# Strassen's seven products for the FFN of the main tokens, with its activations in DRAM and the output projection chunk by chunk

## The chip, the cores and the metric

The kernel runs on one core of a Trainium2 chip, one launch. The metric is device microseconds (us) of that core, the median of three executions. One execution was taken by the hardware profiler; the rows below are from it. The engines are PE (TensorE matmuls; PEld is its weight load), DVE (VectorE), ACT (ScalarE), POOL (GpSimd) and SP (SyncE, which here issues the DMAs).

## What is computed

Two layers of a hybrid block over 1024 main tokens and 256 context tokens, width 1024. Cut to what matters here (g1, sc2, sh2, g2 come from the conditioning vector; the context has its own):

```
x = x + g1 * (y @ w_out[l])                              # y: the three mixers, side by side
h = rms_norm(x, g_ffn[l]) * (1.0 + sc2) + sh2
gate, val = jnp.split(h @ w_up[l], 2, axis=-1)           # 1024 -> 2 x 2816
u = silu(depthwise_conv3(gate) + b) * val                # along the tokens
x = x + g2 * (u @ w_down[l])                             # 2816 -> 1024
# the same for the context tokens, in layer 0 only
```

Ahead of this stands, in each layer, the mixer part: a norm, the combined input projection, neighbourhood attention, differential attention and a Mamba-2 scan.

## The kernel before

Activations lie with their channels on the 128 partitions: 8 blocks of channels, and tokens in three chunks: 0 and 1 (512 main tokens each) and 2 (256 context tokens). Every large product is done at fp32 precision as three matmuls, H·H, L·H and H·L: a tile is rounded to fp32r (H, by a cast) and what is left over is L (by a subtraction). For a weight block, `load_w` does this: an SP DMA into `wr`, the cast on ACT (L240, `wH`), the subtraction on POOL (L241, `wL`).

`outproj` goes chunk by chunk. It reads the mixers' output (already split) from DRAM, does 8 blocks of w_out and adds each into the resident `xt` (DVE, L1278); `norm_sq` sums the squares, and when the chunk is through, `norm_scale` makes the reciprocal root `rs` (a matmul with ones, four ACT steps, two DVE steps) and `norm_apply` makes H and L of the normalised chunk: a multiplication by `rs` on DVE (L364), scale and shift on ACT (L93), the cast on DVE (L369), the subtraction on DVE and POOL in turn (L370).

`ffn` takes two of the 22 blocks of D_FF at a time: gate product (L390 to L392, evacuated by ACT into `fpad`), the convolution on DVE (L1194, L1197), SiLU on ACT, val product and multiplication (L1206), the split into `gh`/`gl` (L1207, L1208), and then the down product of both blocks (L1232 to L1234) for 8 output blocks and each chunk, each added into `xt` by DVE (L1237). So up and down alternate, and each down group of 6 matmuls has a PSUM bank of its own (tag `mm`, 3 banks). The order of instructions on each engine is chosen at build time by the scheduler of the language, not written by hand; each engine then runs its list in order and waits where it must.

In the last pair of layer 0 the next layer's norm follows chunk by chunk.

Of the kernel before, what the change touches and what calls it, by code (L numbers as in the profile page):

```python
# [80 lines left out]
def hybrid_kernel(ctx, tc, xin, cc, w_ada, bada, gmf, w_in, w_dt, w_out, w_up, w_dn, vec, cst, rope, nab, out):  # L81
# [30 lines left out]
    ps_p = ctx.enter_context(tc.tile_pool(name="ps", bufs=1, space=PSUM))  # L112
    mmx = [None, None]

# [6 lines left out]
    open_mm(mm=3)  # L121
# [69 lines left out]
    hp = [None, None]  # L191
    w_pre = []

    def open_h(nm):
        hp[0] = ExitStack()
        hp[1] = hp[0].enter_context(tc.tile_pool(name=nm, bufs=1, side="right", reuse_waits="tile"))

# [6 lines left out]
    hxp = [None, None]  # L204

    def open_hx(nm):
        hxp[0] = ExitStack()
        hxp[1] = hxp[0].enter_context(tc.tile_pool(name=nm, bufs=1, side="right", reuse_waits="tile"))
        new_hx()

    def new_hx():
        for k in range(HX, KT):
            hH[k][0] = hxp[1].tile([128, 512], F32R, tag=f"hxH{k}", name=f"hH{k}_0")
            hL[k][0] = hxp[1].tile([128, 512], F32R, tag=f"hxL{k}", name=f"hL{k}_0")

    def new_h(ci=None, y=False):
        h_p = hp[1]
        for i, (_, n) in enumerate(ALLC):
            if ci is None or ci == i:
                if i == 0 and hxp[1] is not None and not y:  # L220
                    new_hx()
                for k in range(KT if i or hxp[1] is None else HX):
                    hH[k][i] = h_p.tile([128, n], F32R, tag=f"hH{k}_{i}", name=f"hH{k}_{i}")
                    hL[k][i] = h_p.tile([128, n], F32R, tag=f"hL{k}_{i}", name=f"hL{k}_{i}")
# [22 lines left out]
    def pst(tag, bufs):  # L247
        return ps_p.tile([128, 512], F32, tag=tag, name=tag, bufs=bufs)
# [23 lines left out]
    def ada_finish(l, s, k0, nk, pa, pool=None):  # L272
        pm = pa[:, 256:512] if nk == 2 else pst("t", 2)
        for k in range(nk):
            if k % 2 == 0:
                row = (pool or const).tile([128, 256], F32, tag="arow", name="arow", bufs=2 if pool else 1)
# [18 lines left out]
    def ada_native(pool, todo):  # L295
# [11 lines left out]
        for i, (l, s, e) in enumerate(todo):  # L307
# [8 lines left out]
            ada_finish(l, s, 2 * e, 2, pa)  # L316
# [13 lines left out]
    def norm_temps(pool):  # L330
        tl = lambda nm, n=512: pool.tile([128, n], F32, name=nm)
        return dict(acc=[tl(f"acc{i}", n) for i, (_, n) in enumerate(ALLC)], sq=[tl("sq0"), tl("sq1")],
                    rv=tl("rv"), nt=[tl(f"nt{i}") for i in range(4)])
# [19 lines left out]
    def norm_apply(tmp, l, i, xt, ci, rs=None):  # L353
# [6 lines left out]
        for k in range(KT):  # L360
            t = tmp["nt"][k % len(tmp["nt"])][:, :n]
            xv = xt[k][:, c0:c0 + n]
            if not scaled:
                V.tensor_tensor(out=t, in0=xv, in1=rs, op=ALU.mult)  # L364
                xv = t
# [117 lines left out]
    def mixer(l):  # L483
# [66 lines left out]
        with phase(f"sw{l}") as sp:  # L550
# [58 lines left out]
          if True:  # L609
# [558 lines left out]
    def ffn(l, xt):  # L1168
        full = l == 0
        chunks = ALLC if full else MAINC  # L1170
        last = l == NL - 1
        with phase(f"ffn{l}") as p:
# [4 lines left out]
            W = 1282 if full else 1024  # L1177

            def gate_ev(f):
                pad = pads[f % 2]  # L1180

                def ev(ps, c0, n):
                    o = 1 + c0 if c0 < SEQ else 1027
                    S.copy(out=pad[:, o:o + n], in_=ps)  # L1184

                return ev

            def up(f, gate_done=False):
                pad = pads[f % 2]
                if not gate_done:  # L1190
                    proj(w_up[l, 2 * f], chunks, gate_ev(f))
                a = p.tile([128, 1282], F32, tag="fa", name="fa", bufs=1)
                fw = V_FW + 3 * f
                V.tensor_scalar(out=a[:, :W], in0=pad[:, 0:W], scalar1=vcol(l, fw), scalar2=vcol(l, V_FB + f),  # L1194
                                op0=ALU.mult, op1=ALU.add)
                for j in range(1, 3):
                    V.scalar_tensor_tensor(out=a[:, :W], in0=pad[:, j:j + W], scalar=vcol(l, fw + j), in1=a[:, :W],  # L1197
                                           op0=ALU.mult, op1=ALU.add)
                act(out=a[:, :W], in_=a[:, :W], func=ACTF.Silu)
                gh = p.tile([128, T], F32R, tag="gh", name="gh", bufs=3)  # L1200
                gl = p.tile([128, T], F32R, tag="gl", name="gl", bufs=3)

                def evv(ps, c0, n):
                    o = c0 if c0 < SEQ else 1026
                    t = a[:, o:o + n]
                    V.tensor_tensor(out=t, in0=t, in1=ps, op=ALU.mult)  # L1206
                    S.copy(out=gh[:, c0:c0 + n], in_=t)  # L1207
                    G.tensor_tensor(out=gl[:, c0:c0 + n], in0=t, in1=gh[:, c0:c0 + n].bitcast(F32),  # L1208
                                    op=ALU.subtract)

                proj(w_up[l, 2 * f + 1], chunks, evv)
                return gh, gl

            def down(f0, hid, fin):
                tmp = None
                if fin and not last:
                    e0 = p.tile([128, T], F32R, tag="gh", name="gh", bufs=3).bitcast(F32)
                    e1 = p.tile([128, T], F32R, tag="gl", name="gl", bufs=3).bitcast(F32)
                    fa = p.tile([128, 1282], F32, tag="fa", name="fa", bufs=1)
                    tmp = dict(acc=[pads[0][:, 0:512], pads[0][:, 512:1024], pads[1][:, 0:256]],  # L1220
                               sq=[pads[1][:, 256:768], pads[1][:, 768:1280]], rv=fa[:, 0:512],
                               nt=[e0[:, 0:512], e1[:, 0:512], e0[:, 512:1024], e1[:, 512:1024]])
                ws = [load_w(w_dn[l, (f0 + i) * 128:(f0 + i + 1) * 128, :]) for i in range(len(hid))]
                steps = [(o, c) for o in range(KT) for c in chunks]
                if fin:
                    steps = [(o, c) for c in chunks for o in range(KT)]
                for o, (c0, n) in steps:
                    os_ = slice(o * 128, (o + 1) * 128)
                    ps = mmt()[:, :n]
                    for i, (gh, gl) in enumerate(hid):  # L1230
                        wh, wl = ws[i]
                        PE.matmul(ps, wh[:, os_], gh[:, c0:c0 + n], start=(i == 0), stop=False)  # L1232
                        PE.matmul(ps, wh[:, os_], gl[:, c0:c0 + n], start=False, stop=False)  # L1233
                        PE.matmul(ps, wl[:, os_], gh[:, c0:c0 + n], start=False, stop=(i == len(hid) - 1))  # L1234
                    w = 1 if c0 >= SEQ else 0
                    xv = xt[o][:, c0:c0 + n]
                    V.scalar_tensor_tensor(out=xv, in0=ps, scalar=mods[l][:, 5, o, w:w + 1], in1=xv,  # L1237
                                           op0=ALU.mult, op1=ALU.add)
                    if fin and last:
                        SP.dma_start(out=out[o * 128:(o + 1) * 128, c0:c0 + n], in_=xv)  # L1240
                    elif fin:
                        ci = c0 // 512
                        if o == 0 and ci == 0:
                            exp_tables()
                        norm_sq(tmp, ci, o, xv)
                        if c0 < SEQ:
                            SP.dma_start(out=xd[o, :, c0:c0 + n], in_=xv)
                        if o == 1 and ci > 0:
                            norm_apply(tmp, l + 1, 0, xt, ci - 1)
                if fin and not last:  # L1250
                    norm_apply(tmp, l + 1, 0, xt, 2)
# [202 lines left out]
```

## Time and profile before

| what | value |
|---|---|
| device time, median of 3 (range) | 3625.64 us (3623.48 to 3633.13) |
| span of the profiled execution | 3627.4 us |
| PE busy | 3433.8 us (95%), 18762 matmuls |
| PEld busy | 2724.3 us (75%) |
| DVE busy | 1950.4 us (54%) |
| ACT busy | 1242.3 us (34%) |
| POOL busy | 1446.3 us (40%) |
| DMA | 381.03 MB, mean 105 GB/s |

The profile gives no other time of the profiled execution than its span; it is 1.8 us above the median. The FFN of layer 0 runs from about 1080 to 1960 us, that of layer 1 from about 2900 to the end. A busy share is a mean over stages: PE's 95% is 100% in the FFN and less in the mixers and at the joints between the stages.

### The profile page before, as it was taken

To read this page: it belongs to the slowest core of one execution; us is meant where nothing else is said; L and a number is where in the kernel's file an instruction comes from. 1 tells how busy PE (TensorE), PEld (TensorE's weight loads), DVE (VectorE), ACT (ScalarE), POOL (GpSimd) and SP (SyncE) were. 2 spreads that over 40 slices of the span, in tenths; PEclk is the share of its full clock that TensorE was granted. 3 is DMA by queue.
4 is the path that set the end of the run, shared out by engine and by line. 5 is a ranking of instruction groups with operands and counts; after the bars stand their busy time and mean duration, and the time that the engine had idled before them with its cause. 6 is when DMAs were issued, how large, how long until landed. Compare 5 with 4: busy or idle time off the path is not lost. (4 is left out here: it accounts for less than half of the span.)

```text
span 3627.4 us, 49090 instructions
## 1 busy us (share of the span) xinstructions
PE 3433.8 (95%) x18762; PEld 2724.3 (75%) x18762; DVE 1950.4 (54%) x3816; ACT 1242.3 (34%) x2159; POOL 1446.3 (40%) x1092
## 2 busy tenths in 40 slices
PE   7998898899899999999999898998999999999999
PEld 3876676666678888888887676776666777887887
DVE  6735875787373343333335744885784633334333
ACT  4232433777341111111113333344675421221211
POOL 2136563666362222222222326673565532322332
PEclk8999999999999999999999999998999999999999
DMA  8255444753721111111112236447656211111111
GB/s 294 98 199 164 131 126 132 191 152 105 244 83 46 35 41 35 37 39 36 35 35 82 69 114 211 128 128 192 167 156 215 77 53 41 53 47 41 53 47 70
DMA packets 260202, 381.03 MB, mean 105 GB/s; under 512 B 20736, under 2 KB 161152, under 8 KB 259712
## 3 DMA queue, kind: packets, MB, share of 16 engines
q1 hardware_dynamic: 259968, 377.90, 33.8%
q8 instruction: 148, 2.42, 0.3%
q14 instruction: 86, 0.70, 0.1%
HBM read 294.72 MB, written 83.10 MB: 104 GB/s over the span
## 5 line engine op out<-in xcount | busy, mean ns | idle before, releaser
L390 PE MATMUL mm<-hH,wH 128*128 128x512 f32 (+1 forms) x2960 | 1117.6, 379 | 34.2 <-ACT wH L240 7.6
L391 PE MATMUL mm<-hL,wH 128*128 128x512 f32 (+1 forms) x2960 | 1113.2, 376 | 9.5 <-POOL hL L370 5.3
L392 PE MATMUL mm<-hH,wL 128*128 128x512 f32 (+1 forms) x2960 | 1111.4, 376 | 6.2 <-POOL wL L241 6.2
L241 POOL TENSOR_TENSOR wL<-wr,wH 128x1024 fp32r<-128x1024 f32 x220 | 533.2, 2429 | 1218.4 <-ACT wH L240 1195.3
L390 PEld LDWEIGHTS mm<-hH,wH 128*128 128x128 f32 x2960 | 564.7, 191 | 157.6 <-issue 15.1
L391 PEld LDWEIGHTS mm<-hL,wH 128*128 128x128 f32 x2960 | 564.4, 191 | 127.4 <-POOL hL L370 7.8
L392 PEld LDWEIGHTS mm<-hH,wL 128*128 128x128 f32 x2960 | 564.4, 191 | 114.8 <-POOL wL L241 7.7
L240 ACT CAST wH<-wr 128x1024 fp32r<-128x1024 f32 x220 | 228.3, 1048 | 808.1 <-PE mm L1233 471.9
L1237 DVE SCALAR_TENSOR_TENSOR xt<-mm,mods,xt 128x512 f32<-128x512 f32 (+1 forms) x440 | 300.9, 697 | 253.6 <-PE mm L1234 253.1
L1194 DVE TENSOR_SCALAR fa<-fpad,vc 128x1282 f32<-128x1282 f32 (+1 forms) x44 | 111.1, 2526 | 558.6 <-ACT fpad L1184 550.9
L1234 PE MATMUL mm<-gh,wL 128*128 128x512 f32 (+1 forms) x880 | 328.9, 374 | 0.0
L1232 PE MATMUL mm<-gh,wH 128*128 128x512 f32 (+1 forms) x880 | 325.0, 375 | 3.7 <-DVE xt L1237 3.6
L1233 PE MATMUL mm<-gl,wH 128*128 128x512 f32 (+1 forms) x880 | 326.9, 372 | 0.0
L720 DVE TENSOR_SCALAR_CACHE_REDUCE e<-s 128x512 f32<-128x512 f32 (+1 forms) x400 | 228.4, 588 | 88.2 <-PE s L719 85.6
L1208 POOL TENSOR_TENSOR gl<-fa,gh 128x512 fp32r<-128x512 f32 (+1 forms) x110 | 127.6, 1160 | 300.7 <-ACT gh L1207 300.7
L93 ACT ACTIVATE e<-e,nm 128x1280 f32<-128x1280 f32 (+1 forms) x144 | 182.9, 1271 | 53.6 <-DVE nm L723 48.5
L719 PE MATMUL s<-ks,qst 128*128 128x512 f32 (+1 forms) x400 | 161.5, 441 | 39.0 <-DVE e L720 23.4
L1232 PEld LDWEIGHTS mm<-gh,wH 128*128 128x128 f32 x880 | 164.5, 188 | 41.1 <-DVE xt L1237 8.7
L738 POOL TENSOR_TENSOR e<-e 128x1280 f32<-128x1280 f32 (+1 forms) x72 | 193.1, 2684 | 3.4
L1233 PEld LDWEIGHTS mm<-gl,wH 128*128 128x128 f32 x880 | 165.3, 188 | 32.7 <-issue 0.2
L1234 PEld LDWEIGHTS mm<-gh,wL 128*128 128x128 f32 x880 | 165.5, 188 | 32.1
L1206 DVE TENSOR_TENSOR fa<-fa,mm 128x512 f32<-128x512 f32 (+1 forms) x110 | 69.8, 635 | 209.3 <-PE mm L392 151.7
(269 smaller groups left out, 4930.1 us busy)
## 6 DMA issues: line engine op xcount, KB each, us to landing
wr<-in_w_up_dram SPq DMA_DIRECT2D x88, 512.0 KB
wa<-in_w_ada_dram SPq DMA_DIRECT2D x56, 512.0 KB
wr<-in_w_in_dram SPq DMA_DIRECT2D x48, 512.0 KB
wr<-in_w_dn_dram SPq DMA_DIRECT2D x44, 512.0 KB
wr<-in_w_ada_dram SPq DMA_DIRECT2D x40, 512.0 KB
wr<-in_w_out_dram SPq DMA_DIRECT2D x40, 512.0 KB
nbt<-in_nab_dram SPq DMA_DIRECT2D x64, 192.0 KB
ks<-qkd SPq DMA_DIRECT2D x16, 640.0 KB
```

The costliest lines, as they stand in the source:

```text
L93: ins = S.activation(**kw)
L240: S.copy(out=wh, in_=wr)
L241: (eng or G).tensor_tensor(out=wl, in0=wr, in1=wh.bitcast(F32), op=ALU.subtract)
L390: PE.matmul(ps[:, :n], wh[:, ks], r, start=(i == 0), stop=False)
L391: PE.matmul(ps[:, :n], wh[:, ks], hsl(hL, k, c0, n), start=False, stop=False)
L392: PE.matmul(ps[:, :n], wl[:, ks], r, start=False, stop=(i == KT - 1))
L720: V.tensor_scalar(out=e[:, c:c + n], in0=s_, scalar1=1.0, scalar2=None, op0=ALU.mult, op1=ALU.max, accum_out=mx[:, ci:ci + 1])
L738: G.tensor_tensor(out=es[0][:, 0:nk], in0=es[0][:, 0:nk], in1=es[1][:, 0:nk], op=ALU.add)
L1232: PE.matmul(ps, wh[:, os_], gh[:, c0:c0 + n], start=(i == 0), stop=False)
L1233: PE.matmul(ps, wh[:, os_], gl[:, c0:c0 + n], start=False, stop=False)
L1234: PE.matmul(ps, wl[:, os_], gh[:, c0:c0 + n], start=False, stop=(i == len(hid) - 1))
L1237: V.scalar_tensor_tensor(out=xv, in0=ps, scalar=mods[l][:, 5, o, w:w + 1], in1=xv, op0=ALU.mult, op1=ALU.add)
```

## The change

For the main tokens the products are blocked two by two. In the up product the operands are the normalised activations, split into channels 0 to 511 and 512 to 1023 by tokens of chunk 0 and chunk 1 (B11, B21, B22 and the combinations T1 to T4), and two weight blocks half a D_FF apart (combinations s1 to s4, made on DVE). Seven products of 4 blocks replace eight (`up_pair`): 84 matmuls of 512 columns for what took 96. The sums behind the products are DVE additions from PSUM. The context's rows are still done directly (`ctx_rows`).

The FFN is no longer interleaved. `ffn_up` does all up products of a layer and writes the hidden activations and their four combinations to DRAM (`hdd`, 256 KB each; `hcd` for the context). `ffn_down` then does the seven products over 11 blocks, in groups of 4, 4 and 3: each step reads one block back from `hdd` (`br`), splits it (ACT, POOL), splits a combination of the raw weights `wd` (POOL, every fourth on DVE) and issues 12 matmuls into four banks. The residual goes to DRAM (`x1d`) in `outproj` and is read back into `xt` at the start of `ffn_down`. The norm ahead of the FFN (`ffn_norm`) makes the combinations of the activations as well. The first tap of the convolution moves from DVE to ACT.

By the order of instructions, the number of matmuls falls by 792 (396 in each layer, all of 512 columns). Other counts, before and after: DVE tensor-tensor 693 and 1337, DVE scalar-tensor-tensor 1156 and 956, ACT casts 441 and 855, POOL tensor-tensor 632 and 1006, SP DMAs 1320 and 1752.

The core of the diff (new functions):

```diff
+    def up_pair(l, b0, b1, ctx_on, sp, dest):
+        r1 = load_raw(w_up[l, b0])
+        r2 = load_raw(w_up[l, b1])
...
+        ah, al = wpair()
+        split2(ah, al, r1, S, G)
...
+        V.tensor_tensor(out=s1, in0=A21, in1=A22, op=ALU.add)
+        V.tensor_tensor(out=s2, in0=s1, in1=A11, op=ALU.subtract)
+        bh, bl = wpair()
+        split2(bh[:, 0:512], bl[:, 0:512], s2, S, G)
...
+        W, X, Z = mmt(), mmt(), mmt()
+        prod(W, ah, al, 0, "B11", True, False)
+        p1 = tmp("p1")
+        S.copy(out=p1, in_=W)
+        prod(X, bh, bl, 0, "T2", True, False)
+        u2 = tmp("u2")
+        V.tensor_tensor(out=u2, in0=X, in1=p1, op=ALU.add)
+        prod(W, ah, al, 512, "B21", False, True)
+        dest(0, 0, W, None)
+        if ctx_on:
+            dest(0, 2, ctx_rows(ah, al), None)
+        prod(X, bh, bl, 512, "T3", False, False)
+        u3 = tmp("u3")
+        V.tensor_tensor(out=u3, in0=X, in1=p1, op=ALU.add)
+        prod(Z, ch, cl, 0, "T1", True, False)
+        dest(1, 1, Z, u3)
+        prod(X, dh, dl, 512, "T4", False, True)
+        dest(1, 0, X, p1)
...
+        prod(Z, ch, cl, 512, "B22", False, True)
+        dest(0, 1, Z, u2)
...
+                for gi, grp in enumerate(groups):
+                    fin = gi == len(groups) - 1
...
+                            SP.dma_start(out=raw[kt, h], in_=w_dn[l, (kt + h * NP) * 128:(kt + h * NP + 1) * 128, :])
+                    if gi == 0:
+                        for c0, n in chunks:
+                            for o in range(KT):
+                                SP.dma_start(out=xt[o][:, c0:c0 + n], in_=x1d[l][o, :, c0:c0 + n])
...
+                    def product(ps, nm, weight, first, end):
+                        w = None
+                        for i, kt in enumerate(grp):
+                            br = p.tile([128, 512], F32, tag="br", name="br", bufs=3)
+                            SP.dma_start(out=br, in_=hdd[l][BN.index(nm), kt])
+                            xh, xl = [p.tile([128, 512], F32R, tag=f"b{x}", name=f"b{x}", bufs=3) for x in "HL"]
+                            split2(xh, xl, br, S, G)
...
+                            split2(wh, wl, weight(kt), S, sub_eng())
+                            for j in range(4):
+                                js = slice(j * 128, (j + 1) * 128)
+                                mm3(ps[j], wh[:, js], wl[:, js], xh, xl, first and i == 0, end and i == len(grp) - 1)
...
+        else:
+            for k in range(4):
+                t0, t1 = modulated(k), modulated(k + 4)
+                put("B22", k, t1, S, V)
+                d = tmp["tt"]()
+                G.tensor_tensor(out=d, in0=t1, in1=t0, op=ALU.subtract)
+                put("T3", k, d, S, G)
+                h_, l_ = [x.bitcast(F32) for x in bo["B11", k]]
+                V.tensor_tensor(out=t0, in0=t0, in1=h_, op=ALU.subtract)
+                V.tensor_tensor(out=t0, in0=t0, in1=l_, op=ALU.subtract)
+                put("T1", k, t0, S, V)
+                V.tensor_tensor(out=t1, in0=t1, in1=t0, op=ALU.subtract)
+                put("T2", k, t1, S, V)
+                h_, l_ = [x.bitcast(F32) for x in bo["B21", k]]
+                V.tensor_tensor(out=t0, in0=h_, in1=t1, op=ALU.subtract)
+                V.tensor_tensor(out=t0, in0=t0, in1=l_, op=ALU.add)
+                put("T4", k, t0, S, G)
...
-                    V.scalar_tensor_tensor(out=xv, in0=ps, scalar=mods[l][:, 5, o, w:w + 1], in1=xv,
-                                           op0=ALU.mult, op1=ALU.add)
```

How it stands in the engines' lists, at three places.

DVE in layer 1, from `rs` of chunk 1 to the first work of the FFN. Before, the last rows of `norm_apply` and then the first convolution:

```order
L382 SCALAR_TENSOR_TENSOR acc_24990<-rv,acc_24990 128x512
L364 TENSOR_TENSOR nt_24995<-xt_0_24978,acc_24990 128x512
...
L369 CAST hH_1_25680<-nt_24995 128x512
L369 CAST hH_1_25682<-nt_24996 128x512
L370 TENSOR_TENSOR hL_1_25681<-nt_24995,hH_1_25680 128x512
...
L370 TENSOR_TENSOR hL_1_25693<-nt_24997,hH_1_25692 128x512
L1194 TENSOR_SCALAR fa<-fpad_25732,vc 128x1024
```

Now the last rows of `ffn_norm` and then the first weight combinations (`ws`, s1 and s2) of the first `up_pair`:

```order
L412 SCALAR_TENSOR_TENSOR acc_25899<-rv,acc_25899 128x512
L1511 TENSOR_TENSOR xo<-xo,acc_25899 128x512 x8
L1219 TENSOR_TENSOR B220L<-xo,B220H 128x512
...
L1537 TENSOR_TENSOR xo<-xo 128x512
L1219 TENSOR_TENSOR T13L<-xo,T13H 128x512
L1541 TENSOR_TENSOR xo<-xo,B212L 128x512
L1540 TENSOR_TENSOR xo<-B213H,xo 128x512
L1219 TENSOR_TENSOR T23L<-xo,T23H 128x512
L1541 TENSOR_TENSOR xo<-xo,B213L 128x512
L1237 TENSOR_TENSOR ws<-wr 128x512
L1238 TENSOR_TENSOR ws<-ws,wr 128x512
```

Between `rs` and the first convolution DVE had 8 multiplications, 8 casts and 4 subtractions; between `rs` and s2 it now has 8 multiplications, 32 tensor-tensor instructions and s1, and the product T2 needs s2 and T2's operands. In layer 0 the list is the same, with the context's rows (evacuations, squares, norm) between.

PE in the up part of layer 1 (the numbers tell PSUM tiles apart). Before, a down group ends in one bank and the next begins in another:

```order
L1233 MATMUL mm_26464<-gl_26325,wH_26396 128x512
L1234 MATMUL mm_26464<-gh_26324,wL_26397 128x512
L1232 MATMUL mm_26472<-gh_26197,wH_26390 128x512 [waits DVE_49]
L1233 MATMUL mm_26472<-gl_26198,wH_26390 128x512
L1234 MATMUL mm_26472<-gh_26197,wL_26391 128x512
```

Now the product T3 ends in the bank in which T4 goes on (its first operands lie in `hx6` and `hx7`):

```order
L1210 MATMUL mm_26922<-T33H_26717,wH_26901 128x512
L1211 MATMUL mm_26922<-T33L_26718,wH_26901 128x512
L1212 MATMUL mm_26922<-T33H_26717,wL_26902 128x512
L1210 MATMUL mm_26922<-hx6H_26641,wH_26917 128x512 [waits DVE_49,Activation_49]
L1211 MATMUL mm_26922<-hx6L_26642,wH_26917 128x512
L1212 MATMUL mm_26922<-hx6H_26641,wL_26918 128x512 [waits Pool_49]
```

The wait on DVE is for u3, which reads the bank between the two products. In layer 0 the list has the context's 24 matmuls or T1 between T3 and T4.

SP at the passage from up to down in layer 1. Before, weights of both come in turn:

```order
L233 DMA wr<-in_w_up_dram 128x1024 x4
L233 DMA wr<-in_w_dn_dram 128x1024 x2
L233 DMA wr<-in_w_up_dram 128x1024 x4
L233 DMA wr<-in_w_dn_dram 128x1024 x2
L1240 DMA out_dram<-xt_0_24978 128x512
```

Now the last activations go out (`hdd`), then 8 loads of `wd`, 16 of `xt`, and behind them the first `br`:

```order
L258 DMA wr<-in_w_up_dram 128x1024
L1341 DMA hdd_110<-fa 128x512 x3
L1341 DMA hdd_110<-tt 128x512 x4
L1410 DMA wd<-in_w_dn_dram 128x1024 x8
L1414 DMA xt_0_29907<-x1d_114 128x512
...
L1414 DMA xt_7_29914<-x1d_114 128x512
L1440 DMA br<-hdd_110 128x512 x3
```

The first `wd` waits for the landing of the last of the four `tt` writes, since it takes their place in SBUF. In layer 0 five `wd` loads stand ahead of the T writes, and two to five loads of the context's blocks (`hcr`) and six of `br` ahead of the 24 loads of `xt`.

## Rows read from the trace of the kernel before

**Rows 1.** Windows of the FFN: busy us (count) per engine, PE clock, DMA share.

```profile
core 0: us, PE busy (x) PEld busy (x) DVE busy (x) ACT busy (x) POOL busy (x), PEclk, DMA share, GB/s
1100.00:1200.00 100.00, 100.00 (x511) 84.25 (x510) 37.12 (x44) 19.58 (x27) 26.83 (x17) 1.00 0.12 38
...
3300.00:3400.00 100.00, 100.00 (x430) 80.28 (x429) 37.01 (x36) 20.82 (x27) 29.63 (x16) 1.00 0.16 48
```

**Rows 2.** Timeline of PE and DVE, layer 1, down part.

```profile
3005.86 0.40 PE L1234 MATMUL mm<-gh,wL 128*128 128x512 f32 x1
...
3006.30 0.75 DVE L1237 SCALAR_TENSOR_TENSOR xt<-mm,mods,xt 128x512 f32<-128x512 f32 x1 [0.65 <-PE mm L1234]
```

**Rows 3.** Groups by line and shape, 3000 to 3100 us.

```profile
L241 POOL TENSOR_TENSOR wL<-wr,wH 128x1024 fp32r<-128x1024 f32 x9 | 21.5, 2401 | 61.7 <-ACT wH L240 61.7
...
L1208 POOL TENSOR_TENSOR gl<-fa,gh 128x512 fp32r<-128x512 f32 x4 | 5.2, 1292 | 11.6 <-ACT gh L1207 11.6
...
L1206 DVE TENSOR_TENSOR fa<-fa,mm 128x512 f32<-128x512 f32 x4 | 2.8, 688 | 8.0 <-PE mm L392 5.6 <-ACT fa L93 2.4
L1207 ACT CAST gh<-fa 128x512 fp32r<-128x512 f32 x4 | 2.5, 617 | 1.5 <-DVE fa L1206 1.5
```

**Rows 4.** Windows at the norm ahead of the FFN, layer 0 (columns as Rows 1).

```profile
1020.00:1040.00 20.00, 19.28 (x153) 18.29 (x151) 12.79 (x14) 11.07 (x16) 12.15 (x6) 1.00 0.47 149
1040.00:1060.00 20.00, 15.24 (x76) 13.45 (x76) 20.00 (x26) 9.95 (x15) 13.78 (x7) 0.83 0.24 79
1060.00:1080.00 20.00, 17.87 (x71) 14.20 (x71) 11.28 (x24) 7.70 (x15) 8.93 (x13) 0.91 0.16 52
```

**Rows 5.** Timeline of the norm in layer 0: rs, multiplications, POOL beside them.

```profile
1021.57 0.74 DVE L1278 SCALAR_TENSOR_TENSOR xt<-mm,mods,xt 128x512 f32<-128x512 f32 x1
...
1036.99 0.68 DVE L382 SCALAR_TENSOR_TENSOR acc<-rv,acc 128x512 f32<-128x512 f32 x1
...
1037.92 4.64 DVE L364 TENSOR_TENSOR nt<-xt,acc 128x512 f32<-128x512 f32 x4
1038.54 2.87 POOL L241 TENSOR_TENSOR wL<-wr,wH 128x1024 fp32r<-128x1024 f32 x1 [2.42 <-ACT wH L240]
...
1042.82 0.47 DVE L1278 SCALAR_TENSOR_TENSOR xt<-mm,mods,xt 128x256 f32<-128x256 f32 x1
```

**Rows 6.** Timeline of the norm in layer 1: last evacuation, rs, PE's waits.

```profile
2873.06 0.74 DVE L1278 SCALAR_TENSOR_TENSOR xt<-mm,mods,xt 128x512 f32<-128x512 f32 x1
...
2883.01 0.69 DVE L382 SCALAR_TENSOR_TENSOR acc<-rv,acc 128x512 f32<-128x512 f32 x1
...
2883.74 2.50 DVE L364 TENSOR_TENSOR nt<-xt,acc 128x512 f32<-128x512 f32 x4
...
2886.63 0.80 PE L390 MATMUL mm<-hH,wH 128*128 128x512 f32 x1 [2.91 <-DVE hH L369]
...
2890.56 0.79 PE L391 MATMUL mm<-hL,wH 128*128 128x512 f32 x1 [1.35 <-POOL hL L370]
```

**Rows 7.** Windows of PE's low clock there, and at the next mixer's start.

```profile
2886.00:2897.00 11.00, 8.82 (x19) 5.51 (x19) 9.85 (x17) 5.39 (x8) 6.81 (x4) 0.53 0.00 0
...
1980.00:2040.00 60.00, 41.84 (x156) 29.76 (x155) 50.03 (x96) 30.17 (x50) 28.85 (x20) 0.83 0.15 50
```

**Rows 8.** Window of dense DMA in the kernel (columns as Rows 1).

```profile
925.00:950.00 25.00, 20.21 (x79) 15.89 (x78) 5.38 (x8) 6.47 (x9) 7.77 (x4) 0.86 1.05 400
```

**Rows 9.** One 512 KB load: its issue, and GB/s in 3020 to 3024 by tenths.

```profile
3020.17 0.33 SPq L233 DMA_DIRECT2D wr<-in_w_up_dram  x1
...
GB/s 0 0 0 0 0 0 0 0 0 0 0 246 205 328 123 0 41 246 123 205 287 287 369 287 614 328 369 532 246 205 123 82 0 0 0 246 287 41 0 0
```

**Rows 10.** Timeline of POOL and DVE side by side in the FFN, layer 1.

```profile
3029.63 2.40 POOL L241 TENSOR_TENSOR wL<-wr,wH 128x1024 fp32r<-128x1024 f32 x1 [7.13 <-ACT wH L240]
3030.15 2.43 DVE L1194 TENSOR_SCALAR fa<-fpad,vc 128x1024 f32<-128x1024 f32 x1 [11.90 <-ACT fpad L1184]
```

More of the change, by code (lines that the diff above doesn't have):

```diff
@@ L111, in hybrid_kernel @@
     w_p = ctx.enter_context(tc.tile_pool(name="w", bufs=3))
[L112 removed]
     mmx = [None, None]
+    psx = [None, None]
     def open_mm(**bufs):
@@ L119, in open_mm, with open_ps @@
         mmx[1] = mmx[0].enter_context(tc.tile_pool(name="mm", bufs=1, space=PSUM, reuse_waits="tile")), bufs
-    open_mm(mm=3)
+    def open_ps(**mm):
+        if mmx[0] is not None:
+            mmx[0].close()
+            mmx[0] = None
+        if psx[0] is not None:
+            psx[0].close()
+        psx[0] = ctx.enter_context(ExitStack())
+        psx[1] = psx[0].enter_context(tc.tile_pool(name="ps", bufs=1, space=PSUM, reuse_waits="tile"))
+        if mm:
+            open_mm(**mm)
+    open_ps(mm=3)
     dr = ctx.enter_context(tc.tile_pool(name="dr", bufs=1, space=DRAM))
@@ L327, in side_finish, with norm_temps @@
             pass
-    def norm_temps(pool):
+    def norm_temps(pool, own=True, nt=True):
         tl = lambda nm, n=512: pool.tile([128, n], F32, name=nm)
-        return dict(acc=[tl(f"acc{i}", n) for i, (_, n) in enumerate(ALLC)], sq=[tl("sq0"), tl("sq1")],
-                    rv=tl("rv"), nt=[tl(f"nt{i}") for i in range(4)])
+        a0, a1 = tl("acc0"), tl("acc1")
+        d = dict(acc=[a0, a1, tl("acc2", CTX) if own else a1[:, 0:CTX]], sq=[tl("sq0"), tl("sq1")], rv=tl("rv"))
+        if nt:
+            d["nt"] = [tl(f"nt{i}") for i in range(4)]
+        return d
     def norm_sq(tmp, ci, k, xv):
@@ L1165, in natt, with mm3 @@
             yield
-    def ffn(l, xt):
+    hdd = [dr.tile([7, NF // 2, 128, 512], F32, name=f"hdd{l}") for l in range(NL)]
+    hcd = [dr.tile([NF, 128, CTX], F32, name=f"hcd{l}") for l in range(NL)]
+    x1d = [dr.tile([KT, 128, T], F32, name=f"x1d{l}") for l in range(NL)]
+    BN = ("B11", "B21", "B22", "T1", "T2", "T3", "T4")
+    def mm3(ps, wh, wl, bh, bl, first, last):
+        PE.matmul(ps, wh, bh, start=first, stop=False, skip_group_check=True)
+        PE.matmul(ps, wh, bl, start=False, stop=False, skip_group_check=True)
+        PE.matmul(ps, wl, bh, start=False, stop=last, skip_group_check=True)
@@ L1169, in ffn, with ffn_up @@
+    def ffn_up(l):
         full = l == 0
-        chunks = ALLC if full else MAINC
-        last = l == NL - 1
-        with phase(f"ffn{l}") as p:
+        with phase(f"up{l}") as p:
             pads = [p.tile([128, 1284], F32, name=f"fpad{i}") for i in range(2)]
@@ L1214, in down @@
[L1214 to L1236, printed above, removed]
-                    V.scalar_tensor_tensor(out=xv, in0=ps, scalar=mods[l][:, 5, o, w:w + 1], in1=xv,
[L1238 to L1251, printed above, removed]
@@ new lines, in ffn_norm, with modulated, put @@
+    def ffn_norm(l, tmp, xs, ci):
+        n = ALLC[ci][1]
+        w = 1 if ci == 2 else 0
+        rs = norm_scale(tmp, ci)
+        def modulated(k):
+            t = xs[k]
+            V.tensor_tensor(out=t, in0=t, in1=rs, op=ALU.mult)
+            act(out=t, in_=t, func=ACTF.Identity, scale=amod[l][:, 1, k, w:w + 1], bias=mods[l][:, 3, k, w:w + 1])
+            return t
+        def put(nm, k, src, he, le):
+            bo[nm, k] = op_tile(nm, k)
+            split2(*bo[nm, k], src, he, le)
+        if ci == 2:
+            for k in range(KT):
+                hc[k] = pair_tile(hp[1], f"c{k}", CTX)
+                split2(*hc[k], modulated(k), V, G if k % 2 else V)
+        elif ci == 0:
+            for k in range(KT):
+                put(("B11", "B21")[k // 4], k % 4, modulated(k), V, G if k % 2 else V)
+        else:
+            for k in range(4):
+                t0, t1 = modulated(k), modulated(k + 4)
[13 more added lines that the diff above has]
+                put("T4", k, t0, S, G)
```

347 lines of the change are left out of this document (264 added, 83 removed).

## The prediction, as it was put on record

> **What bounds the kernel now.** I read the page's busy shares first (PE 95%), then the windows, since a share is a mean over stages. In the FFN PE is busy 100 of 100 us at full clock, with DVE at 37%, POOL at 27 to 30% and DMA at 0.12 to 0.16 [rows 1]. Matmuls alone set the pace there: 430 of 512 columns in 100 us, 0.233 us each; and in layer 0, where a third have 256 columns, 511. A group's evacuation starts 0.44 us after its last matmul starts, takes 0.75 us and lies beside the next group, which has its own bank [rows 2]. PE loses time only at joints. At the norm of layer 0 it idles 7.6 of the 60 us from 1020, and the clock of 0.83 and 0.91 costs some 4.5 more: 12 in all [rows 4]. At the norm of layer 1 it waits 2.91 and 1.35 us, and then does 19 matmuls in 11 us at a clock of 0.53, which is the lower level (1.2 GHz) for nearly all of it [rows 6, 7]: 19 matmuls need 4.4 us, so the whole loss there is about 9 with the idle, some 4 of it clock. At the start of the next mixer 18 of 60 us are idle, at a clock of 0.83 [rows 7].
>
> **What it removes.** 792 matmuls of 512 columns at 0.233 us [rows 1]: −184.8 us. All stand where PE is the bound, so each counts, as long as PE stays fed. What follows is the price of feeding it.
>
> **A, C: the norm ahead of the FFN.** The product T2 waits for everything that DVE has ahead of s2. *Layer 1 (C).* From the last evacuation's start (2873.06) to `rs` (2883.70) are 10.6 us [rows 6]; that chain is kept. Then come 8 + 32 + 2 tensor-tensor instructions of 512; the four at 2883.74 took 0.625 each, and with PSUM or a late operand 0.69: 42 × 0.64 = 27 us. POOL meanwhile has 12 instructions of 512 (four differences, four lows each of T3 and T4) at 1.2 to 1.29 [rows 3], 14.4 us. How far the two lie side by side: four multiplications that took 2.50 alone [rows 6] took 4.64 beside a POOL subtraction of 2.87 [rows 5], so three quarters of POOL's time was added to DVE's. That gives 27 + 0.75 × 14.4 = 38 us, and 2 more for s2's cast and low [rows 3]. PE's cover is B11 and B21, 24 matmuls, 5.6 us. Idle: 10.6 + 38 + 2 − 5.6 = 45; then 4 at low clock as before; less the 9 lost now: +40. Bounds: 29 (no hindrance at all) to 46 (POOL's time added in full, longer low clock). *Layer 0 (A).* `rs` of chunk 1 ends 16.1 us after its last evacuation's start (1021.57 to 1037.67) [rows 5], and the matmul with ones stands at the same place in PE's list after the change. DVE then has 40 tensor-tensor (25.8 us), six of the context's evacuations and square sums (0.47 and about 0.41 [rows 5], 5.3), the context's norm (9, as halves of the 512 durations) and s1, s2 (1.3): 40 us alone. POOL has 22 us, so 40 + 0.75 × 22 = 56. PE's cover is larger: the context's w_out (192 matmuls of 256 columns, 23 us), B11, B21 and the context's rows, 31.5. 16.1 + 56 + 2 − 31.5 + 4 − 12 = +35 (18 with no hindrance, 43 with all of it and a stall in the context's norm).
>
> The Trainium skill, "SBUF — State Buffer", section "Who interferes with whom", goes further than the row of three quarters: a DVE instruction with two SBUF inputs and a POOL one that reads SBUF shut each other out entirely, the later waiting for the end of the earlier. The trace agrees in kind: a DVE instruction that began 0.52 us after a POOL one of 2.40 lasted 2.43, ending 0.55 after it [rows 10]. By that rule the two terms would be 43 and 40 in place of 40 and 35, and the sum 8 higher.
>
> **M: T4 behind T3, layer 1.** Both accumulate in one bank, and u3 reads it between. PE waits from T3's last matmul: 0.44 to u3's start [rows 2] + 0.69 [rows 3] + some 0.07 = 1.20 instead of 0.233, so 0.97 for each of 22 pairs; in half of them one T1 matmul stands between and hides 0.23. +19 (15 to 30, if u3 stands behind other DVE work). In layer 0 the context's rows or T1 hide it: **B** +3 (0 to 20, the price of layer 1).
>
> **E, F: from up to down.** Now weights of both parts come in turn, long ahead. *Layer 1 (E).* After the last up product come an evacuation, a multiplication and four differences on DVE (0.4 + 6 × 0.65 = 4.3 us), the writes' landing (a 512 KB load was issued at 3020.17 and moved bytes until some 3 us later [rows 9]; I take 3), then 8 loads of 512 KB and 16 of 256 KB, 8.4 MB, ahead of the first `br`. The densest stretch moves 400 GB/s [rows 8]: 21 us. `br`'s own 3 us and its cast and low (1.9 [rows 3]) follow: 33 us of idle PE and 4 at low clock, +37. Bounds: 23 (the traffic alone and some clock) to 44 (issues and waits not overlapped). *Layer 0 (F).* Five weight loads and the context's first blocks stand ahead of the 5.2 MB of `xt`; the first step should start 10 to 13 us after up's end, and a later context block behind `xt` (13 us) delays the sixth step by 3 to 7 more. +18 with the clock (10 to 26).
>
> **G: the pace of down.** A step is 12 matmuls, 2.80 us. POOL has one low for `b` and three quarters of one for `w`: 1.75 × 1.25 = 2.2 us; DVE's instructions with two SBUF inputs are 0.82 a step (0.53 us); even one after the other they take 2.73. Only T2's steps (two combinations, 3.6) are over, and the buffers of three take part of it: +8 (0 to 45, with each T2 step a full 0.85 late and gaps between the engines). ACT's two casts (1.2) and 256 KB of DMA in 2.8 us, a quarter of 400 GB/s, are hidden. Up's weights are paced as now: per pair POOL has 10 us and DVE 6.5 under PE's 19.6. The next mixer's norm loses what it loses now (18 us idle), being late in both: 0 (−6 to +6). Evacuations in down (36 of 0.75 in 78 us) lie under the matmuls.
>
> **The sum.** −185 + 35 + 40 + 19 + 3 + 37 + 18 + 8 = −25. The durations are from an execution with a span of 3627.4, 1.8 above the median: 3602 there, 3600 against the median of 3625.6.
>
> **The rivals.** *R1, starts cheap.* DVE and POOL don't hinder each other (busy shares of 37 and 27% speak for it; the 4.64 against 2.50 speaks against), and loads overlap up's end: lower bounds throughout, 18 + 29 + 15 + 0 + 23 + 10 + 0 = 95, −90: 3536. *R2, slower: down is bound by the port that DVE and POOL share.* If handing over costs time, each step takes not 2.73 but 3.3 us, and 154 steps (7 × 11 × 2) lose 0.5 each: 77 instead of 8, 3669. For it: POOL's load in down is 79% of PE's time, against 30% now [rows 1], and its 2.40 became 2.87 beside DVE [rows 5]. Against: full serial time still fits. It is slower than before from a step of 3.01 us (33 us over 154 steps). *R3, no change.* The four starts come at their upper bounds, 43 + 46 + 44 + 26 = 159 instead of 130: 3629. A and C with DVE and POOL strictly one after the other would be a quarter of the way there.
>
> **How the numbers follow.** 0.3% (11 us) is about what a measurement of this kernel can tell from no change: 3615 to 3636. Forecast 3600 (own range 3560 to 3640): 0.42; R1 0.13; R3 0.17; R2 and what else goes beyond it 0.28. The forecast's own spread puts about 0.08 of it into no change, and R3 leaves some 0.05 on the fast side. Faster 0.52, same 0.20, slower 0.28. The range 3535 to 3665 leaves out half of R1 (0.06) and the far side of R2 (0.14).
>
> **What would show it.** In the windows of layer 1's up part, 100 us with PE near 95% and its waits on DVE's u3, about 1 us each; ahead of T2, one wait of 40 us or so, on DVE or the low of s2; at the passage to down one of some 33 us on `br`, with DMA at its full rate; in down, matmuls 0.233 apart. If down's steps take over 3 us with PE waiting for POOL's lows, R2 holds. If the waits at the starts are under 20 us, R1. The prediction is wrong outright if PE waits in up for weights as well, or if matmuls into a bank that the preceding product used cost more than 0.233.

## The result, and the profile after

The changed kernel takes 3681.79 us (median of 4, 3674.3 to 3683.07), the kernel before 3629.05 in the same comparison: ratio 1.0137, 95% interval 1.012 to 1.0155. It is 1.4% slower; the prediction was 3600 us. The profiled execution has a span of 3681.3, 53.9 over that of before.

The page of the changed kernel begins (part 1):

```profile
span 3681.3 us, 50474 instructions
PE 3275.6 (89%) x17970; PEld 2597.1 (71%) x17970; DVE 2298.2 (62%) x4200; ACT 1497.3 (41%) x2595; POOL 1966.4 (53%) x1466
```

PE's busy time did fall, by 158 us, with exactly 792 matmul records less; but its idle time rose from 194 to 406. The waits that hold the most, from its view of waits of PE after 2885 us (layer 1) and from 1030 to 2060 us (layer 0); the columns are the sum in us, the count and the longest:

```profile
PE mm L1210 <- ACT p L1273: 39.3, 1, 39.3
PE A L1210 <- ACT bH L1216: 35.1, 1, 35.1
PE mm L1210 <- DVE u L1283: 22.1, 22, 6.0
...
PE mm L420 <- DVE xo L1565: 29.8, 2, 29.1
PE B L1210 <- ACT hcH L1216: 23.2, 2, 14.5
PE B L379 <- DVE acc L373: 14.3, 2, 12.3
PE mm L420 <- DVE h_0H L399: 11.5, 1, 11.5
```

The first three are the joints that the prediction named for layer 1 (norm, passage to down, T4 behind T3), each within a few microseconds of the wait that it expected. The next two are layer 0's norm and passage. The last two stand at the next mixer's norm. Windows of the changed kernel, in the order layer 0's up, the idle stretch of layer 1's norm, layer 1's up and layer 1's down part (columns as Rows 1):

```profile
1200.00:1250.00 50.00, 50.00 (x261) 42.40 (x261) 24.57 (x31) 16.22 (x21) 22.50 (x14) 1.00 0.24 85
2931.00:2966.00 35.00, 0.00 (x0) 0.00 (x0) 34.12 (x43) 17.33 (x28) 18.71 (x9) 0.50 0.00 0
3050.00:3100.00 50.00, 47.61 (x203) 37.53 (x202) 33.47 (x37) 17.19 (x24) 28.90 (x18) 1.00 0.28 91
3550.00:3650.00 100.00, 100.00 (x443) 82.81 (x442) 70.67 (x80) 41.83 (x74) 89.47 (x65) 1.00 0.44 132
```

So the seven products do run at PE's pace once they run: against [rows 1], full in layer 0's up part and in down. What this doesn't hold is where 40 of the 54 us went. The first evacuation of each output projection (DVE's timeline: start and duration in us, then the instruction, and in brackets the idle time before it), of the kernel before:

```profile
938.76 1.41 DVE L1278 SCALAR_TENSOR_TENSOR xt<-mm,mods,xt 128x512 f32<-128x512 f32 x2 [13.26 <-DMA xt<-in_xin_dram]
2789.52 2.07 DVE L1278 SCALAR_TENSOR_TENSOR xt<-mm,mods,xt 128x512 f32<-128x512 f32 x3 [14.14 <-PE mm L392]
```

and of the changed kernel:

```profile
955.62 2.07 DVE L1565 SCALAR_TENSOR_TENSOR xo<-mm,mods,xo 128x512 f32<-128x512 f32 x3 [17.37 <-PE mm L422]
2838.66 2.07 DVE L1565 SCALAR_TENSOR_TENSOR xo<-mm,mods,xo 128x512 f32<-128x512 f32 x3 [16.90 <-PE mm L422]
```

Layer 0's output projection starts 16.9 us late, ahead of anything that the change was for. From its start to the end of layer 1 the two kernels split thus (us, each the difference of two events in the traces; the tail is the stretch of the two attentions side by side, from its first score matmul):

| stretch | before | after | difference |
|---|---|---|---|
| tail of layer 0's mixer | 326.5 | 342.9 | +16.4 |
| output projection, FFN and next norm, layer 0 | 1186.8 | 1195.1 | +8.3 |
| layer 1's mixer up to its tail | 370.4 | 370.7 | +0.3 |
| tail of layer 1's mixer | 293.6 | 317.2 | +23.6 |
| output projection and FFN, layer 1 | 837.8 | 842.6 | +4.8 |

Up to 650 us every engine's instructions come in the same order in both kernels, to within 3 us of the same times; then, inside the first tail (it begins at 612.3 us before and 612.7 after), the lists part, and 0.5 us of delay grow to 17. The tails hold the same matmuls in another order. In windows a little wider than them, with some 2500 matmuls in layer 0 and 2370 in layer 1, PE was busy 310.6 of 348 us in layer 0 (586 to 934) at a mean clock of 0.97, then 316.5 of 364.4 (586.6 to 951) at 0.94.

### The profile page after: what moved, and what is told of

Same layout as the page of the kernel before. It is cut to its first block, busy times and chain, and to the rows that moved or that the text cites. A ratio compares the mean times of both kernels' runs of the same rounds, so it can differ in the third digit from the quotient of the medians.

```text
span 3681.3 us, 50474 instructions
## 1 busy us (share of the span) xinstructions
PE 3275.6 (89%) x17970; PEld 2597.1 (71%) x17970; DVE 2298.2 (62%) x4200; ACT 1497.3 (41%) x2595; POOL 1966.4 (53%) x1466
## 4 chain that ended last, share of the span: by engine, by line
PE 70%; DVE 11%; DMA 9%; POOL 4%; issue 3%; ACT 2%; SPq 1%; DVEq 0%; ACTq 0%; POOLq 0%
PE mm L1210 8%; PE mm L1211 8%; PE mm L1212 8%; PE mm L421 5%; PE mm L420 5%; PE mm L422 5%; PE B L1211 2%; PE A L1211 2%; PE B L1212 2%; PE B L1210 2%; PE A L1210 2%; PE s L749 2%; PE A L1212 2%; DMA ks<-qkd 2%; PE o L797 2%
## 5 line engine op out<-in xcount | busy, mean ns | idle before, releaser
L266 POOL TENSOR_TENSOR wL<-wr,wH 128x1024 fp32r<-128x1024 f32 x88 | 216.1, 2459 | 391.1 <-ACT wH L265 344.0
L1219 POOL TENSOR_TENSOR wL<-wr,wH 128x1024 fp32r<-128x1024 f32 x88 | 187.6, 2132 | 363.1 <-ACT wH L1216 363.1
L1219 POOL TENSOR_TENSOR wL<-ws,wH 128x512 fp32r<-128x512 f32 x176 | 256.3, 1480 | 107.2 <-ACT wH L1216 105.3
L1219 POOL TENSOR_TENSOR wL<-wd,wH 128x512 fp32r<-128x512 f32 (+1 forms) x122 | 193.3, 1596 | 82.9 <-ACT wH L1216 82.5
L1219 POOL TENSOR_TENSOR bL<-br,bH 128x512 fp32r<-128x512 f32 x154 | 217.7, 1427 | 26.9 <-ACT bH L1216 26.5
L988 POOL TENSOR_SCALAR mf<-cs,lah 128x128 fp32r<-128x128 f32 x288 | 140.7, 505 | 48.8 <-PE s L990 47.0
L1320 DVE SCALAR_TENSOR_TENSOR fa<-fpad,vc,fa 128x1282 f32<-128x1282 f32 (+1 forms) x88 | 137.3, 1608 | 33.1 <-ACT fa L93 33.1
L420 PE MATMUL mm<-h_0H,wH 128*128 128x512 f32 x320 | 135.5, 425 | 19.6 <-DVE h_0H L399 11.5
L1211 PE MATMUL A<-bL,wH 128*128 128x512 f32 x352 | 139.3, 396 | 1.9 <-POOL bL L1219 1.9
L420 PE MATMUL mm<-h_1H,wH 128*128 128x512 f32 x320 | 133.4, 417 | 7.2 <-DVE h_1H L399 5.8
L421 PE MATMUL mm<-h_0L,wH 128*128 128x512 f32 x320 | 132.9, 416 | 7.7 <-DVE h_0L L400 4.9
```

The costliest lines, as they stand in the source:

```text
L266: (eng or G).tensor_tensor(out=wl, in0=wr, in1=wh.bitcast(F32), op=ALU.subtract)
L420: PE.matmul(ps[:, :n], wh[:, ks], r, start=(i == 0), stop=False)
L421: PE.matmul(ps[:, :n], wh[:, ks], hsl(hL, k, c0, n), start=False, stop=False)
L1211: PE.matmul(ps, wh, bl, start=False, stop=False, skip_group_check=True)
L1219: le.tensor_tensor(out=out_l, in0=src, in1=out_h.bitcast(F32), op=ALU.subtract)
```

## The experiments

Theory O: the scheduler, given one small edit, put the tails' instructions in a slower order; the FFN's own costs are the joints. Rival W: something else of the change (reopened PSUM pools, places in SBUF) delays the tails. The traces of the first two runs hold the lists: with the second buffer for `arow` alone, the kernel before has in layer 0's tail the changed kernel's order on PE, DVE, ACT and POOL, row for row; and with a single buffer there the changed kernel has the order of the kernel before.

**The kernel before, with that one line.**

```diff
-                row = (pool or const).tile([128, 256], F32, tag="arow", name="arow", bufs=2 if pool else 1)
+                row = pool.tile([128, 256], F32, tag="arow", name="arow", bufs=2)
...
-            ada_finish(l, s, 2 * e, 2, pa)
+            ada_finish(l, s, 2 * e, 2, pa, pool)
```

> The kernel before with one line of the change: the row tile of the conditioning rows (arow) gets a second buffer, in the pool of the stage that uses it, in place of a single one for the whole kernel. PE's list in the tail of layer 0's mixer then reads word for word as in the changed kernel. Theory O (the scheduler's new order costs the time in the mixers' tails): layer 0's output projection starts some 17 us later than in the kernel before, layer 1's tail changes too, and the whole comes to 3645 to 3675 us. Rival W (the tails wait for something else in the change: PSUM pools that are reopened, places in SBUF): no shift, 3626 to 3634 us.

3660.84 us against 3629.89: ratio 1.0086 (1.0063 to 1.0109). The first evacuation of layer 0's output projection:

```profile
947.65 1.41 DVE L1278 SCALAR_TENSOR_TENSOR xt<-mm,mods,xt 128x512 f32<-128x512 f32 x2 [17.52 <-DMA hH<-ydd]
```

Layer 0's tail takes 341.6 us (+15.1), as in the changed kernel. The output projection starts only 8.9 us late, and not 17, since the stretch ahead of the tail took 606.1 us in place of 612.3 in this execution (604.7 to 612.7 over all runs). In layer 1 the order is another again, and the tail takes 295.4. Layer 0's output projection and FFN take 10 more. These parts come to 21 us: the profiled execution, 3650.44, is the fastest of the four, 10 under their median. Theory O holds for layer 0: 31 us come from a line without one instruction more or less, though not all of them inside the tail.

**The changed kernel with one buffer for arow in the tails.**

```diff
-                row = pool.tile([128, 256], F32, tag="arow", name="arow", bufs=2)
+                row = pool.tile([128, 256], F32, tag="arow", name="arow", bufs=1 if nk == 2 else 2)
```

> The changed kernel with a single buffer for arow in the mixers' tails; PE's list in the tail of layer 0 then reads as in the kernel before. Theory O: layer 0's output projection starts at about 939 us in place of 956, and the whole falls by 17 us, to about 3665 us, plus what the new order of layer 1's tail gives or takes (0 to 23 us less). Rival W: no shift at 956 us, 3675 to 3685 us.

3651.95 us (1.0063, 1.0044 to 1.0082), 30 less than the change.

```profile
943.71 1.41 DVE L1565 SCALAR_TENSOR_TENSOR xo<-mm,mods,xo 128x512 f32<-128x512 f32 x2 [17.57 <-PE mm L422]
```

Layer 0's tail: 331.4; layer 1's, in a third order: 303.5. So W falls for most of the time. Something of it may remain: with the list of before, this tail is 4.9 us longer than in the kernel before, and 5 to 8 longer in the three later runs with that list. Over all runs the tail of layer 0 took 326 to 347 us and that of layer 1 294 to 324, at equal work; the lists of after gave 342 to 347 in layer 0 (339 in one run), those of before 326 to 335. In layer 1, too, the time goes with the list: on DVE four runs have one list (the change, T4 in a bank of its own, T1 between, the context's norm in two pieces) and took 317 to 324 us, and the first two combinations have another and took 301 and 303.

**Loads at the start of down in another order.**

```diff
-                    if gi == 0:
-                        for c0, n in chunks:
-                            for o in range(KT):
-                                SP.dma_start(out=xt[o][:, c0:c0 + n], in_=x1d[l][o, :, c0:c0 + n])
...
                     product(A, "B11", lambda kt: quarter(0, 0, kt), True, False)
+                    xt_loads(MAINC)
...
-                        return raw[kt, j][:, i * 512:(i + 1) * 512]
+                        return raw_load(kt, j)[:, i * 512:(i + 1) * 512]
```

> The changed kernel with the loads at the start of the down part in another order: each weight block wd is loaded ahead of the step that needs it, and the loads of xt follow the first product's. Theory (the 8.4 MB ahead of the first activations make the wait of 35 us in layer 1 and of 14.5 and 8.8 us in layer 0): layer 1's wait falls to 12 to 16 us (evacuation, differences, the write and the read of one block), layer 0's two waits together to under 12 us; some 30 us less in the two passages. Rival (the wait is the chain of the last T4 write and its read back, and the loads lie beside it): layer 1 stays above 28 us.

3656.36 us (1.0079, 1.0056 to 1.0102). Its waits of PE after 3400 us:

```profile
PE A L1210 <- ACT wH L1216: 13.5, 1, 13.5
PE B L1210 <- ACT wH L1216: 8.4, 1, 8.4
```

The 35.1 are 13.5, as expected, but a wait of 8.4 for the next weights comes behind them: the loads are only later, not fewer. In layer 0 the two waits for the context's blocks, 23.2 together, became six, 12.5 in all. Layer 1's FFN takes 6.5 us less, layer 0's 6.7; most of the rest of the 25 came from the tail of layer 1 (305.6, a new order), which this edit was not for. The theory holds for the first wait and not for the gain.

**T4 in a bank of its own (layer 1).**

```diff
-        prod(X, dh, dl, 512, "T4", False, True)
-        dest(1, 0, X, p1)
+            Y = pst("s", 2)
+            prod(Y, dh, dl, 512, "T4", True, True)
+            dest(1, 0, Y, u3)
```

> The changed kernel with T4 of the up part in layer 1 in a bank of its own, added to u3 at its evacuation, so that T4 need not wait until u3 has read T3's bank. Nothing else moves in the lists of the mixers. Theory (the bank makes the wait of 0.65 to 0.88 us a pair, 22 us in all): the waits on u3 go and the kernel takes 18 to 23 us less, 3659 to 3664 us. Rival (DVE is late in any case and PE waits at the next use of a bank): under 8 us less.

3707.61 us (1.0224, 1.0202 to 1.0247): 26 slower than the change. The waits on u3 went, and others came, on B22, which goes on in T1's bank; its view of waits of PE has:

```profile
PE mm L1210 <- DVE fpad L1315: 30.9, 10, 3.1
```

and a window of 50 us among them:

```profile
3050.00:3100.00 50.00, 46.88 (x194) 36.99 (x193) 31.68 (x33) 14.59 (x21) 27.01 (x17) 0.97 0.27 91
```

Ten waits of 3.1 us, and the clock in such windows falls to 0.97, where the 0.9 us waits of the change left it at 1.00: fewer, longer waits cost idle time and clock. The rival's mechanism was right, PE waits for DVE at the next use of a bank; that it would cost 26 us was foreseen by neither.

**T1 between T3 and T4**, by a tie without a semaphore:

```diff
+            tc.add_manual_dep(t1[0].ins, t3[-1].ins.name, nosync, reason="order")
...
+            tc.add_manual_dep(t4[0].ins, t1[-1].ins.name, nosync, reason="order")
```

> The changed kernel with one order on PE in layer 1's up part: T3, then T1, then T4 (T4's first matmul is tied behind T1's last, without a semaphore). The lists of the mixers stay. Theory (u3 needs only 1 us, and 12 matmuls cover it): the waits on u3 fall from 22 us to the 6 us of the first pair, the whole to 3662 to 3668 us. Rival (DVE's list is late for every evacuation, as it showed for B22 when T4 had a bank of its own): the waits go to another product, and the time stays above 3674 us.

3690.87 us (1.0174, 1.0159 to 1.0189), no gain: the 22 waits became eleven on u3, one of 3.3 us and ten of some 1.85, 21.8 us in all in place of 22.1. DVE's timeline shows what is late:

```profile
3064.31 4.23 SPq L1348 DMA_DIRECT2D hdd<-tt  x3
...
3066.40 1.79 DVE L1362 TENSOR_TENSOR tt<-fa 128x512 f32<-128x512 f32 x1 [0.74 <-DMA hdd<-tt]
...
3070.42 2.28 DVE L1365 TENSOR_TENSOR tt<-fa,tt 128x512 f32<-128x512 f32 x1 [2.23 <-DMA hdd<-tt]
3072.62 0.68 DVE L1285 TENSOR_TENSOR u<-mm,p 128x512 f32<-128x512 f32 x1
```

u3 stands behind the fourth combination `tt`, and that waits for a write to DRAM: there are two `tt` buffers for four tiles.

**The context's norm in two pieces**, its matmul with ones later:

```diff
-                        norm_next(2)
+                        norm_next(2, True, False)
...
                     to(A, [(0, 0)], (0, 0))
+                    if fin and not last:
+                        norm_next(2, False, True)
```

> The changed kernel with the context's norm for the next mixer in two pieces: the squares where they are, the matmul with ones and what follows it behind the product B21 of the last group. Theory (PE stands 12.3 us at 1947 because the matmul with ones waits in its list for the square sums on DVE): this wait goes, layer 0 takes 10 to 14 us less, 3668 to 3672 us. Rival (DVE is what is late there, and the evacuations behind it wait instead): under 5 us less.

3686.42 us (1.0163, 1.0146 to 1.018). The 12.3 us wait of the matmul with ones became one of 17.3 further on: DVE's backlog there is the cause, not the matmul's place. A miss.

**All lows of down's weights on POOL.**

```diff
-                    return V if cnt[0] % 4 == 0 else G
+                    return G
```

> The changed kernel with all lows of the weights in the down part on POOL, in place of every fourth on DVE: POOL has 2 x 1.29 = 2.58 us a step and DVE's combinations 0.37, against 2.72 us of matmuls. Theory of the shared port (what DVE takes is added to POOL): a step takes 2.95 us, PE waits for lows of POOL in the down windows, some 25 to 35 us over both layers. Rival (they lie side by side): no such waits.

3671.53 us in one run (layer 1's tail in another order, so the total says little). In 110 us of layer 1's down part:

```profile
3530.00:3640.00 110.00, 109.76 (x476) 89.92 (x475) 57.81 (x73) 43.24 (x76) 103.56 (x78) 0.98 0.43 126
```

POOL is busy 103.6 us and PE still waits only 0.2 us for it, and 0.4 us in the down parts of both layers together. Even so loaded, the port that DVE and POOL share doesn't bound down; the prediction's rival R2 is out.

**POOL's part of the norm on DVE.**

```diff
-                G.tensor_tensor(out=d, in0=t1, in1=t0, op=ALU.subtract)
-                put("T3", k, d, S, G)
+                V.tensor_tensor(out=d, in0=t1, in1=t0, op=ALU.subtract)
+                put("T3", k, d, S, V)
...
-                put("T4", k, t0, S, G)
+                put("T4", k, t0, S, V)
```

> The changed kernel with POOL's 12 instructions in the norm of chunk 1 (the difference for T3, the lows of T3 and T4) on DVE. Theory of the shared port (a DVE instruction with two SBUF inputs and a POOL one take turns, the later waits 1.07 us): DVE gains 12 x 0.62 = 7.4 us of work and loses 8.6 us of turns, and POOL's low of 6.41 us, behind which ACT's copy of p1 stands, goes: the wait ahead of T2 in layer 1 changes by -4 to +1 us from 39.3. Rival (the two lie side by side and DVE's list alone counts): +7 us, 46 us.

3665.84 us (1.0099, 1.0085 to 1.0114). The wait ahead of B21 and T2 falls from 39.3 to 35.6: twelve instructions more on DVE, and it is through 3.7 us earlier. The first wait on u3 behind it falls from 6.0 to 2.4, and layer 1 from its output projection on takes 832.0 us, 10.6 less. In the changed kernel one sees why:

```profile
2957.88 0.68 DVE L1535 TENSOR_TENSOR xo<-xo,B113L 128x512 f32<-128x512 f32 x1
...
2959.90 6.41 POOL L1219 TENSOR_TENSOR hx6L<-xo,hx6H 128x512 fp32r<-128x512 f32 x1 [7.30 <-ACT hx6H L1216]
...
2964.51 0.68 DVE L1237 TENSOR_TENSOR ws<-wr 128x512 f32<-128x512 f32 x1
...
2966.34 0.59 ACT L1273 COPY p<-mm 128x512 f32<-128x512 f32 x1 [1.10 <-POOL hx6L L1219]
...
2967.57 1.75 DVE L1238 TENSOR_TENSOR ws<-ws,wr 128x512 f32<-128x512 f32 x1 [2.38 <-POOL hx7L L1219]
```

A DVE instruction that meets one of POOL's takes 1.75 in place of 0.68, and one of POOL's that meets a run of DVE's takes 6.41 in place of 1.29: it gets through at the first break of DVE's list, and ACT's copy of p1, which B21 needs, stands behind it. The profiled execution, 3679.64, is the slowest of the four, so the 16 us between the medians are not accounted for in full.

**Together.** First arow, late loads, T1 between and the split context norm:

> The changed kernel with four edits together: one buffer for arow in the tails, the later loads in the down part, T1 between T3 and T4, and the context's norm in two pieces. From the parts: 3682 less 30, 13 in the FFN, 16 and 11: about 3612 us, 0.5% under the kernel before; with the order of layer 1's tail open by 15 us either way. Rival (the waits replace each other at the joints): 3640 us or more.

3639.61 us (1.0031, 1.0017 to 1.0045): practically the rival's figure. The third and the fourth had given nothing by themselves. Then without the fourth, and with the ring that DVE had waited for made longer:

```diff
-                    return p.tile([128, 512], F32, tag="tt", name="tt", bufs=2)
+                    return p.tile([128, 512], F32, tag="tt", name="tt", bufs=2 if full else 4)
```

> The changed kernel with one buffer for arow in the tails, the later loads in the down part, T1 between T3 and T4, and in layer 1 four buffers in place of two for the combinations tt that go to DRAM (the context's norm as in the change). In the run with T1 between T3 and T4 alone, u3 stood on DVE behind the last tt, which waited for the landing of an earlier write. Theory (the ring of two tt holds DVE up): the waits of 1.85 us on u3 go, layer 1 from its output projection on takes 816 to 822 us in place of 836, the whole about 3620 us. Rival (DVE is late for other reasons): 832 us or more, 3635 us or more.

3616.34 us (0.9966, 0.9954 to 0.9979). Layer 1 from its output projection on takes 817.2 us, 19 less than in the combination before and 20.6 less than in the kernel before. Its waits on u2 (L1278) and u3 (L1285):

```profile
PE mm L1210 <- DVE u L1278: 6.1, 11, 0.9
PE mm L1210 <- DVE u L1285: 2.7, 1, 2.7
```

So the ring held u3 up. Whether the longer ring alone would do, without T1 between, wasn't run. Last, with the norm on DVE and, in layer 1, early weights (and two buffers in place of three for the blocks that are read back):

```diff
+                    pre[kt] = pre["pool"].tile([128, 512], F32, name=f"wp{kt}")
+                    SP.dma_start(out=pre[kt], in_=w_dn[l, kt * 128:(kt + 1) * 128, 0:512])
```

> The kernel of the combination with four tt buffers, the norm of chunk 1 on DVE alone, and in layer 1 the weights of the first product loaded during the up part into a pool of their own, with two buffers for the activations there. PE's lists in both mixers' tails read nearly as in the kernel before. From the parts: 3640 less 16 (tt), 5 to 10 (first weights early) and 0 to 8 (tail of layer 1): 3606 to 3620 us, 0.2 to 0.6% under the kernel before. Rival (what is saved at one joint is waited for at the next): 3630 us or more.

3606.39 us against 3627.66: 0.9938 (0.9926 to 0.9951), faster than both kernels. The passage to down in layer 1 costs 5.6 (in two waits) and 9.3 us in place of 35.1, and layer 1's tail 297.9. Against the kernel before, the stretch from the output projection on (in layer 0 through the next norm) is 3.8 us shorter in layer 0 and 22.4 in layer 1, and the two tails are 8.0 and 4.3 longer.

## Why the prediction was wrong

- *−184.8 for 792 matmuls.* Right: full windows in the FFN, at 0.233 us in up. In down they come every 0.227 (443 records in 100 us against 430), 11 us more over 1848 matmuls, which the prediction did not have.
- *C, layer 1's norm, +40.* Measured +32 up to T2; +41 only together with the first wait on u3, which belongs to M. What is measured is a stretch less 0.233 us for each of its matmuls, so that low clock counts too: 42.4 us from the last evacuation's start (2924.28) to 2980, against 10.2 before [rows 6, 7], and 8.9 more from there to 2995, around the wait on u3. The path was right in the main: DVE was busy 34.1 of 35 us, and T2 started 48.0 us after the last evacuation, where the sum has 10.6 + 38 + 2. But T2's neighbour B21 waited too, for ACT's copy of p1, so not all of the 5.6 us of cover was there. The "three quarters" of POOL's time turned out as 9 of 42 instructions at 1.75 us, 1.07 more each. These are nearly full turns, as the Trainium skill has it ("SBUF — State Buffer", "Who interferes with whom"), for those that met, while others of POOL's were put off instead. In [rows 5], too, the turn was full: of the four multiplications three took 0.68 us and one 2.83, ending 0.54 after POOL's. The instruction of [rows 10] has one SBUF tensor as its input (it takes 0.81 us where no POOL instruction overlaps), so it shows such a wait, but not one of two inputs.
- *A, layer 0's norm, +35.* Measured 50.8 against 13.2 [rows 4]: +37.6, most of it in one wait of 29.1 for a bank, whose evacuation stood in DVE's list behind the norm.
- *M, +19.* 22 waits, 22.1 us, of which the first pair 6.0; some 25 with the low clock behind that one. The place was right and the size nearly. The reading "0.44 + 0.69" was good for the single wait (0.65 to 0.88), but that twelve matmuls of cover would remove it was an assumption (experiments four and five): behind it stood the ring of two `tt`. B, +3: none measured.
- *E, +37.* Measured 37.8, 35.1 of it in one wait. *F, +18.* Mis-sized: 29.5, in two waits of 14.5 and 8.8 and low clock.
- *G, +8, and the rival R2.* Down's steps have two waits of 3.0 us at the heads of groups in layer 0 (the context's lows), one of 2.0 in layer 1, and otherwise only the norm's waits below and some of 1.4 or less; 2.72 us a step. R2 was wrong, and that its 3669 lies nearest to the measured time is luck.
- *"The next mixer's norm loses what it loses now: 0."* Failed. The context's norm put a wait of 12.3 into the last group (15.3 with the low clock behind it), and the start of the mixer loses 41 us in place of 31: some +25, from DVE's backlog of squares, combinations and evacuations (moving the matmul moved the wait).
- *No term for the mixers.* This is the step that failed most, and it was not written: the sum put the mixers' tails, whose code hardly changes, at nothing without a reason. They gave +40. The edit of `arow` is in the change, costs no instruction, and reorders two stretches of 300 us each; the prediction read the order at three joints and not there. Without the tails the FFN and its joints come to +13, against −25. The difference is the norm of the next mixer (+25), F (+11), M (+6) and the output projections, for which there was no term either (+7: 12.9 and 11.0 us lost up to their last evacuations of the main tokens, in place of 8.7 and 8.4), less C (−8) and down's faster matmuls (−11); the rest is in smaller terms.

What stays open: why the one order of the tails is slower than the other. No single wait holds it: in layer 0's windows PE's idle time grew by some 10 us, in waits of 7 us and less, and its busy time by 6 at the lower clock. Open, too, are the 5 to 8 us by which the changed kernel's tail is longer even with the old list. And the runs with four changes don't separate what each gave in the total, since layer 1's tail came in a new order in most of them; its length is the main scatter between variants.

## What to carry to other kernels

Where a scheduler sets the order, compare the lists of all stages, the untouched ones above all, before a gain is forecast, and where they differ leave that stretch's time open: one more buffer for a tile of 1 KB on each partition cost 31 us, a sixth of what the matmuls saved. A saving at a saturated engine is worth its full size only between joints; each new stage boundary (norm ahead of combined operands, write and read back through DRAM) cost 30 to 40 us here. When a wait is removed, look for what the late engine itself waits for: once the bank no longer held PE, a ring of two buffers ahead of a DRAM write did.

## What was not expected of the hardware

- Matmuls of 512 columns follow each other every 0.233 us in up and every 0.227 in down, at the same granted clock of 1.00. In down PE's list goes through four banks with one activation tile; whether that is the cause wasn't tried.
- A POOL subtraction of 1.29 us lasted 6.41 while DVE had a run of instructions with two SBUF inputs without a break.
- Of the two levels of the clock, 1.2 and 2.4 GHz, a stretch of 50 us with waits of 0.9 us some 20 us apart shows a mean of 1.00 (only the higher one); one with waits of 3.1 us some 44 us apart shows 0.97.
